# Hyena long convolution on one Trainium2 core: the sums of the filter products moved from GpSimd to VectorE, and the even tiles' products fed from PSUM

## The chip, the cores and the metric

The kernel runs on one core of a Trainium2 chip. The core has a matrix engine (TensorE, PE in the profile; its weight loads are PEld), a vector engine (VectorE, DVE), a scalar engine (ScalarE, ACT), a general engine (GpSimd, POOL) and a queue engine (SyncE, SP) that issues almost all DMA transfers. Each engine works through its own instructions in a fixed order and waits for others on semaphores. The metric is the device time of one execution in microseconds (us).

## The reference, cut to what matters

The program is one encoder block: two token mixers side by side (an S5 state space model and a Hyena operator), merged by gates, then a SwiGLU channel mixer. The change lies in the Hyena operator:

```python
def _fft_conv(z, kf, bias):
    zf = jnp.fft.rfft(zf32, n=2 * seq, axis=1)
    y = jnp.fft.irfft(zf * kf[None], n=2 * seq, axis=1)[:, :seq]
    return (y + zf32 * bias.astype(jnp.float32)).astype(z.dtype)
...
    z = v
    for o in range(HY_ORDER):
        z = gates[o] * _fft_conv(z, kf[:, o], bias[o])
```

The sequence has 1024 positions, there are 512 Hyena channels and two orders, and all is float32. What matters is the product `zf * kf` of a complex spectrum with a complex filter spectrum: for each frequency two real numbers times two real numbers, four products and two sums.

## The kernel before, in words

The Fourier transforms are matrix products on PE. The 512 channels are two halves of 256 columns (`hyena_half`, L505). Each half runs `long_conv` (L480) twice, once per order. A generator per half yields after each step, and `side_by_side` (L535) takes the two in turn, so that one half's waits can be covered by the other. The tile framework then orders the instructions of each engine by priority and by its own timeline of costs (`schedule_with_timeline_sim=True`), so the order on an engine is not the order of the source.

One `long_conv` does this:

* `fold` (L278) adds and subtracts rows of the signal until its even and odd parts can be transformed apart. It uses VectorE, GpSimd (L308, L309, L316, L317, L325, L326) and ScalarE.
* For the four even frequency tiles (7, 6, 4, 5), `spectrum` (L366) makes the tile's real and imaginary part by two to four matmuls into one PSUM tile of [128, 2, 256], named `sp`. There is one such PSUM buffer for each half. ScalarE copies it to the SBUF tile X (L487), and `times_filter` (L460) multiplies it with the filter spectrum `kt`, which SP loads from DRAM (L464, two buffers).
* `times_filter` works on X in SBUF. VectorE makes t2, the two parts crossed times the filter's imaginary part (L466, t in the profile), and X times the filter's real part in place (L473; for tile 7 two halves, L470 and L471). GpSimd then makes the two sums, each [128, 256], into Y (L475 and L476). Y is the input of the inverse transform's matmuls (L413 and L428 through L362), or of `butterfly` (L379) for odd tiles.
* For the odd tiles (0 to 3), `spectrum_odd` (L391) copies one PSUM tile to X (L399) and combines it with a second one out of PSUM on VectorE (L384, L385, L388). `times_filter` then works on X as above, and `butterfly` makes g from two Y tiles.
* `combine_odd` (L440) transforms back and joins the parts, with GpSimd at L454 and L457 and VectorE at L450 and L456.

After each order the result is multiplied with a gate (L517, L529, L530). Over two halves and two orders there are 16 even and 16 odd products, thus 64 sums.

During the Hyena stage the other engines' spare time is filled with two pieces that do not need its result: the gate projections `emit_gates_b` (L1244, PE tile gp) and the S5 branch `emit_branch_a` (L1301, PE tile br, VectorE L1318, weights split by ScalarE L135 and GpSimd L136 into wh and wl). When both halves are done, `emit_merge` (L1329) runs the Hyena branch projection, also named br.

Of the kernel before, what the change touches and what calls it, by code (L numbers as in the profile page):

```python
# [11 lines left out]
ALU = mybir.AluOpType  # L12
# [4 lines left out]
P = 128  # L17
# [336 lines left out]
def transform(E, out, offs, rhs, start, stop, shared=False):  # L354

    n = len(offs)
    if len(rhs[0]) == 2:
        lhs = [(E.dft_hi[:, o:o + P], E.dft_lo[:, o:o + P]) for o in offs]
        mm3(E, out, lhs, rhs, start, stop, shared)
        return  # L360
    for i in range(n):
        E.nc.tensor.matmul(out=out, lhsT=c32(E, offs[i]), rhs=rhs[i][0], start=start and i == 0,  # L362
                           stop=stop and i == n - 1, skip_group_check=shared)


def spectrum(E, sp, ft, parts):  # L366

    out = sp()
    for i in range(2):
        z = parts["even"][i]  # L370
        if ft < 6:
            offs, tiles = [A2_OFF + 256 * kt + P * (ft - 4) for kt in range(2)], range(2)
        else:
            offs, tiles = [M_OFF + P * ((A1, D2), (S4, S2))[i][ft - 6]], [ft - 4]
        transform(E, out[:, i], offs, [tuple(t[:, k] for t in z) for k in tiles], True, True)
    return out


def butterfly(E, out, a, b, special, eng):  # L379

    STT = E.nc.vector.scalar_tensor_tensor
    if special:
        e = col(E.tab, T_E)
        STT(out=out[0], in0=b, scalar=e, in1=a, op0=ALU.mult, op1=ALU.add)  # L384
        STT(out=out[1], in0=a, scalar=e, in1=b, op0=ALU.mult, op1=ALU.subtract)  # L385
    else:
        for o, op in zip(out, (ALU.add, ALU.subtract)):
            eng.tensor_tensor(out=o, in0=a, in1=b, op=op)  # L388


def spectrum_odd(E, sp, k, parts, out):  # L391

    for m in range(2):
        pt = sp()
        for i in range(2):
            transform(E, pt[:, i], [A5_OFF + 512 * m + 256 * n + P * k for n in range(2)],
                      [tuple(t[:, 2 * m + n] for t in parts["odd"][i]) for n in range(2)], True, True)
        if m == 0:
            E.nc.scalar.copy(out[1], pt)  # L399
        else:  # L400
            butterfly(E, out, out[1], pt, k == 0, E.nc.vector)


def combine_even(E, room, inv, product):

    nc = E.nc
    TT = nc.vector.tensor_tensor
    banks = []
    for ft, mats in ((7, (D2T, S2T)), (6, (A1, S4))):
        Y = product(ft)  # L410
        bank = inv("EA")
        for i in range(2):
            transform(E, bank[:, i], [M_OFF + P * mats[i]], [(Y[:, i],)], i == 0, i == 1, True)  # L413
        banks.append(bank)
        yield
    m4 = room("fq", [P, 2, 256], "m4")
    nc.scalar.copy(m4, banks[1])
    m3 = room("t2", [P, 2, 256], "m3", bufs=2)
    nc.scalar.copy(m3, banks[0])
    G = [room("g", [P, 2, 256], "G", bufs=4) for _ in range(2)]  # L420
    nc.gpsimd.tensor_tensor(out=G[0], in0=m3, in1=m4, op=ALU.add)
    TT(out=G[1], in0=m3, in1=m4, op=ALU.subtract)
    EC, ES = inv("EC"), inv("ES")
    for kt in range(2):
        Y = product(4 + kt)
        for bank, i in ((EC, 0), (ES, 1)):
            for t in range(2):
                transform(E, bank[:, t], [A2_OFF + 256 * kt + P * t], [(Y[:, i],)],  # L428
                          kt == 0 and t == 0, kt == 1 and t == 1, True)
        yield  # L430
    ce, so = room("ze", [P, 4, 256], "ce"), room("fw", [P, 4, 256], "so")
    for n in range(2):
        TT(out=ce[:, n], in0=EC[:, n], in1=G[n][:, 0], op=ALU.add)
        TT(out=ce[:, 3 - n], in0=G[n][:, 0], in1=EC[:, n], op=ALU.subtract)
        TT(out=so[:, 2 * n], in0=ES[:, 1 - n], in1=G[n][:, 1], op=ALU.add)
        TT(out=so[:, 3 - 2 * n], in0=ES[:, 1 - n], in1=G[n][:, 1], op=ALU.subtract)
    return ce, so


def combine_odd(E, room, inv, g, ce, so, y):  # L440

    V = E.nc.vector
    for i, z in enumerate((so, ce[:, 3::-1])):
        U, W = inv("U"), inv("W")
        for m, bank in enumerate((U, W)):
            for n in range(2):
                transform(E, bank[:, n], [A5T_OFF + 512 * m + 256 * k + P * n for k in range(2)],
                          [(g[k][m][:, i],) for k in range(2)], n == 0, n == 1, True)
        for out, own, other, t in ((z[:, 0:2], U, W, T_NTAN), (z[:, 3:1:-1], W, U, T_TAN)):
            V.tensor_tensor(out=out, in0=own, in1=out, op=ALU.add)  # L450
            tmp = room("t2", [P, 2, 256], "tw", bufs=2)
            for n in range(2):
                E.nc.scalar.mul(tmp[:, n], other[:, n], col(E.tab, t + n))
            E.nc.gpsimd.tensor_tensor(out=out, in0=out, in1=tmp, op=ALU.add)  # L454
        yield
    V.tensor_tensor(out=y[:, 0:4], in0=ce, in1=so, op=ALU.add)  # L456
    E.nc.gpsimd.tensor_tensor(out=y[:, 7:3:-1], in0=ce, in1=so, op=ALU.subtract)  # L457


def times_filter(E, room, X, o, hf, ft):  # L460

    nc = E.nc
    kt = room("kt", [P, 2, 256], bufs=2)
    nc.sync.dma_start(out=kt, in_=E.kspec[o, hf, ft, :, 0:2])  # L464
    t2 = room("t2", [P, 2, 256], bufs=2)
    nc.vector.tensor_tensor(out=t2, in0=X[:, ::-1], in1=kt[:, 1:2].to_broadcast([P, 2, 256]), op=ALU.mult)  # L466
    if ft == 7:
        k2 = room("k2", [P, 256])
        nc.sync.dma_start(out=k2, in_=E.kspec[o, hf, ft, :, 2])
        nc.vector.tensor_tensor(out=X[:, 0], in0=X[:, 0], in1=kt[:, 0], op=ALU.mult)  # L470
        nc.vector.tensor_tensor(out=X[:, 1], in0=X[:, 1], in1=k2, op=ALU.mult)  # L471
    else:
        nc.vector.tensor_tensor(out=X, in0=X, in1=kt[:, 0:1].to_broadcast([P, 2, 256]), op=ALU.mult)  # L473
    Y = room("Y", [P, 2, 256], bufs=2)
    nc.gpsimd.tensor_tensor(out=Y[:, 0], in0=X[:, 0], in1=t2[:, 0], op=ALU.add)  # L475
    nc.gpsimd.tensor_tensor(out=Y[:, 1], in0=X[:, 1], in1=t2[:, 1], op=ALU.subtract)  # L476
    return Y


def long_conv(E, room, inv, sp, T, o, hf, out):  # L480

    parts = fold(E, room, T, T)
    yield

    def even(ft):
        X = room("t1", [P, 2, 256], "X", bufs=2)
        E.nc.scalar.copy(X, spectrum(E, sp, ft, parts))  # L487
        return times_filter(E, room, X, o, hf, ft)

    ce, so = yield from combine_even(E, room, inv, even)  # L490
    g = []
    for k in range(2):
        X = [room("t1", [P, 2, 256], "X", bufs=2) for _ in range(2)]
        spectrum_odd(E, sp, k, parts, X)
        yield
        Y = [times_filter(E, room, X[n], o, hf, 2 * k + n) for n in range(2)]
        g.append([room("g", [P, 2, 256], bufs=4) for _ in range(2)])
        butterfly(E, g[k], *Y, k == 0, E.nc.vector)
        yield
    y = out()  # L500
    yield from combine_odd(E, room, inv, g, ce, so, y)
    return y
# [1413 lines left out]
```

## Time and profile before

| what | value |
|---|---|
| time, median of 3 runs | 1694.34 us (1690.42 to 1696.2) |
| the profiled execution's own time | 1695.38 us |
| span of its trace, first to last instruction | 1693.6 us |
| PE busy | 1539.2 us (91%) |
| VectorE busy | 1316.4 us (78%) |
| ScalarE busy | 743.4 us (44%) |
| GpSimd busy | 577.6 us (34%) |
| TensorE clock granted, mean | 0.966 |

Times in the trace are counted from the span's start. A busy share over the whole span mixes many stages; the Hyena stage lies from about 660 to 866 us. In a list of groups the numbers after the bar are the total busy time in us, the mean duration of one instruction in ns, and the idle time of the engine just before, with what ended it. An instruction that follows another directly on VectorE starts some 0.08 us before the profile ends the one before it, so the sum of durations is larger than the busy time.

### The profile page before, as it was taken

How to read it: one execution, taken by the hardware profiler on the slowest of the kernel's cores; microseconds unless marked ns; L12 is line 12 of the kernel's file. 1: busy time of each engine (PE TensorE's matmuls, PEld its weight loads, DVE VectorE, ACT ScalarE, POOL GpSimd, SP SyncE). 2: the span in 40 equal slices, each digit the busy share in tenths (PEclk: the TensorE clock that was granted, in tenths of full speed). 3: DMA queues.
4: the chain of work that ended last, by engine and by line, in shares of the span. 5: the costliest groups of instructions: out<-in, count | busy, mean ns of one | idle time of the engine just before them, and what ended most of it. 6: DMA issues, size and time to landing. Idle time of an engine off the chain costs nothing. (4 is left out here: it accounts for less than half of the span.)

```text
span 1693.6 us, 22059 instructions
## 1 busy us (share of the span) xinstructions
PE 1539.2 (91%) x7598; PEld 1272.2 (75%) x7598; DVE 1316.4 (78%) x1967; ACT 743.4 (44%) x1366; POOL 577.6 (34%) x393
## 2 busy tenths in 40 slices
PE   6777889899988898997789998999999999999995
PEld 2666768787777786785578997878888888778884
DVE  6889798889999737898887666866776766578966
ACT  5846456435555464223133465433333333345544
POOL 3355663413334347779631120211111111012232
PEclk9998999999999999999989998999999999999998
DMA  9446653353332276754237732423223332598863
GB/s 327 125 139 190 172 168 103 104 153 99 88 86 63 84 207 248 254 168 138 86 126 258 256 95 63 143 81 106 94 93 105 119 126 87 167 372 311 311 205 113
DMA packets 244871, 263.82 MB, mean 156 GB/s; under 512 B 27672, under 2 KB 168816, under 8 KB 243317
## 3 DMA queue, kind: packets, MB, share of 16 engines
q1 hardware_dynamic: 244278, 259.99, 47.8%
q0 software_dynamic: 480, 2.42, 0.4%
q8 instruction: 60, 0.98, 0.2%
q14 instruction: 53, 0.43, 0.1%
HBM read 195.00 MB, written 67.34 MB: 155 GB/s over the span
## 5 line engine op out<-in xcount | busy, mean ns | idle before, releaser
L136 POOL TENSOR_TENSOR wl<-wf,wh 128x1024 fp32r<-128x1024 f32 (+1 forms) x56 | 129.7, 2317 | 227.8 <-ACT wh L135 167.2
L144 PE MATMUL pj<-hT,wh 128*128 128x512 f32 x480 | 193.5, 403 | 9.0 <-ACT cva L1187 8.3
L146 PE MATMUL pj<-hT,wl 128*128 128x512 f32 x480 | 192.3, 401 | 0.5 <-POOL wl L136 0.5
L146 PE MATMUL gu<-h2T,op 128*128 128x512 f32 x440 | 172.6, 393 | 3.8 <-DVE op L136 3.8
L144 PE MATMUL gu<-h2T,op 128*128 128x512 f32 x440 | 171.3, 393 | 4.5 <-ACT op L135 2.5
L136 POOL TENSOR_TENSOR wl<-wg,wh 128x1024 fp32r<-128x1024 f32 x22 | 55.6, 2533 | 346.9 <-ACT wh L135 346.9
L145 PE MATMUL gu<-h2T,op 128*128 128x512 f32 x440 | 172.7, 392 | 0.0
L135 ACT CAST op<-ws 128x512 fp32r<-128x512 f32 x88 | 54.4, 622 | 182.9 <-PE gu L146 109.0
L145 PE MATMUL dn<-dop 128*128 128x512 f32 x308 | 120.8, 392 | 0.3 <-POOL dop L136 0.3
L146 PE MATMUL dn<-dop 128*128 128x512 f32 x308 | 120.7, 392 | 0.0
L144 PEld LDWEIGHTS pj<-hT,wh 128*128 128x128 f32 x480 | 92.7, 193 | 28.4 <-ACT cva L1187 9.0
L144 PE MATMUL dn<-dop 128*128 128x512 f32 x308 | 111.9, 391 | 2.1 <-ACT dop L135 2.1
L146 PEld LDWEIGHTS pj<-hT,wl 128*128 128x128 f32 x480 | 92.6, 193 | 20.5 <-POOL wl L136 1.4
L145 PE MATMUL pj<-hT,wh 128*128 128x512 f32 x256 | 101.1, 395 | 0.0
L144 PEld LDWEIGHTS gu<-h2T,op 128*128 128x128 f32 x440 | 83.5, 190 | 23.4 <-ACT op L135 3.2
L146 PEld LDWEIGHTS gu<-h2T,op 128*128 128x128 f32 x440 | 83.5, 190 | 22.5 <-DVE op L136 5.0
L145 PEld LDWEIGHTS gu<-h2T,op 128*128 128x128 f32 x440 | 83.6, 190 | 17.1
L145 PE MATMUL pj<-lT,wh 128*128 128x512 f32 x224 | 90.8, 405 | 0.0
L136 POOL TENSOR_TENSOR dop<-bf,dop 128x512 fp32r<-128x512 f32 x17 | 32.0, 1884 | 129.5 <-ACT dop L135 120.9
L1538 DVE TENSOR_TENSOR ws<-wu 128x512 f32<-128x512 f32 x22 | 24.7, 1123 | 66.0 <-DMA wu<-in_ffn_w_gu_dram 66.0
L144 PE MATMUL wop<-woh,mT 128*128 128x256 f32 x256 | 73.0, 285 | 1.6 <-DVE tmp L1413 1.6
L145 PE MATMUL wop<-wol,mT 128*128 128x256 f32 x256 | 72.5, 283 | 0.0
(462 smaller groups left out, 4383.8 us busy)
## 6 DMA issues: line engine op xcount, KB each, us to landing
bf<-in_ffn_w_down_dram SPq DMA_DIRECT2D x105, 256.0 KB
wf<-in_w_in_dram SPq DMA_DIRECT2D x36, 512.0 KB
ada<-in_ada_w_dram SPq DMA_DIRECT2D x48, 256.0 KB
wg<-in_ffn_w_gu_dram SPq DMA_DIRECT2D x22, 512.0 KB
wu<-in_ffn_w_gu_dram SPq DMA_DIRECT2D x22, 512.0 KB
adS<-S SPq DMA_DIRECT2D x44, 256.0 KB
af<-adS SPq DMA_DIRECT2D x44, 256.0 KB
adA<-a SPq DMA_DIRECT2D x33, 256.0 KB
```

The lines of the kernel that those rows point to most:

```text
L135: E.nc.scalar.copy(hi, src)
L136: (lo_eng or E.nc.vector).tensor_tensor(out=lo, in0=src, in1=bc(hi), op=ALU.subtract)
L144: E.nc.tensor.matmul(out=out, lhsT=lh, rhs=rh, start=first, stop=False, skip_group_check=shared)
L145: E.nc.tensor.matmul(out=out, lhsT=lh, rhs=rl, start=False, stop=False, skip_group_check=shared)
L146: E.nc.tensor.matmul(out=out, lhsT=ll, rhs=rh, start=False, stop=last, skip_group_check=shared)
L1538: V.tensor_tensor(out=s1, in0=u1, in1=u2, op=ALU.add)
```

## The change

The function `times_filter` gets one more argument, S, from which the products read; X stays the tile that they are written to. For even tiles S is the PSUM tile of `spectrum`, and ScalarE's copy to X is gone. For odd tiles S is X itself, as before. The two sums into Y are issued on VectorE where they were issued on GpSimd.

```diff
-def times_filter(E, room, X, o, hf, ft):
+def times_filter(E, room, S, X, o, hf, ft):
...
-    nc.vector.tensor_tensor(out=t2, in0=X[:, ::-1], in1=kt[:, 1:2].to_broadcast([P, 2, 256]), op=ALU.mult)
+    nc.vector.tensor_tensor(out=t2, in0=S[:, ::-1], in1=kt[:, 1:2].to_broadcast([P, 2, 256]), op=ALU.mult)
     if ft == 7:
...
-        nc.vector.tensor_tensor(out=X[:, 0], in0=X[:, 0], in1=kt[:, 0], op=ALU.mult)
-        nc.vector.tensor_tensor(out=X[:, 1], in0=X[:, 1], in1=k2, op=ALU.mult)
+        nc.vector.tensor_tensor(out=X[:, 0], in0=S[:, 0], in1=kt[:, 0], op=ALU.mult)
+        nc.vector.tensor_tensor(out=X[:, 1], in0=S[:, 1], in1=k2, op=ALU.mult)
     else:
-        nc.vector.tensor_tensor(out=X, in0=X, in1=kt[:, 0:1].to_broadcast([P, 2, 256]), op=ALU.mult)
+        nc.vector.tensor_tensor(out=X, in0=S, in1=kt[:, 0:1].to_broadcast([P, 2, 256]), op=ALU.mult)
     Y = room("Y", [P, 2, 256], bufs=2)
-    nc.gpsimd.tensor_tensor(out=Y[:, 0], in0=X[:, 0], in1=t2[:, 0], op=ALU.add)
-    nc.gpsimd.tensor_tensor(out=Y[:, 1], in0=X[:, 1], in1=t2[:, 1], op=ALU.subtract)
+    nc.vector.tensor_tensor(out=Y[:, 0], in0=X[:, 0], in1=t2[:, 0], op=ALU.add)
+    nc.vector.tensor_tensor(out=Y[:, 1], in0=X[:, 1], in1=t2[:, 1], op=ALU.subtract)
     return Y
...
         X = room("t1", [P, 2, 256], "X", bufs=2)
-        E.nc.scalar.copy(X, spectrum(E, sp, ft, parts))
-        return times_filter(E, room, X, o, hf, ft)
+        return times_filter(E, room, spectrum(E, sp, ft, parts), X, o, hf, ft)
...
-        Y = [times_filter(E, room, X[n], o, hf, 2 * k + n) for n in range(2)]
+        Y = [times_filter(E, room, X[n], X[n], o, hf, 2 * k + n) for n in range(2)]
```

## Rows read from the trace of the kernel before

**Rows 1.** The chain of waits, 560 to 868 us: start us, us, what.

```profile
863.74 1.97 PE yT L526 x8
```

**Rows 2.** Busy time by stretch: PE, PEld, DVE, ACT, POOL (count), PE clock, DMA share, GB/s.

```profile
660.00:866.00 206.00, 174.80 (x738) 140.92 (x737) 176.11 (x215) 54.63 (x111) 152.38 (x124) 0.95 0.52 170
...
700.00:745.00 45.00, 45.00 (x205) 38.36 (x204) 40.67 (x55) 8.36 (x17) 29.44 (x28) 1.00 0.59 192
...
770.00:800.00 30.00, 22.18 (x84) 16.79 (x83) 27.29 (x25) 9.22 (x18) 27.14 (x20) 0.89 0.45 142
800.00:845.00 45.00, 33.47 (x138) 26.14 (x136) 38.98 (x60) 7.15 (x15) 30.54 (x32) 0.95 0.27 82
...
866.00:905.00 39.00, 39.00 (x174) 31.73 (x173) 29.94 (x41) 13.05 (x21) 7.63 (x6) 0.98 0.60 186
```

**Rows 3.** Who waited for whom on DVE, 660 to 866 us: total us, times, longest.

```profile
DVE g L384 <- POOL Y L476: 5.1, 4, 1.7
DVE t L466 <- ACT X L487: 4.7, 3, 2.0
...
DVE g L388 <- POOL Y L476: 2.0, 2, 1.3
DVE t L466 <- POOL Y L476: 1.9, 2, 1.3
...
DVE X L384 <- POOL Y L476: 1.3, 1, 1.3
```

**Rows 4.** Groups, 660 to 866 us: sums, copy; the last row 770 to 800 us.

```profile
L475 POOL TENSOR_TENSOR Y<-X,t 128x256 f32<-128x256 f32 x32 | 30.1, 940 | 26.4 <-DVE X L473 24.8 <-DVE X L470 1.6
L476 POOL TENSOR_TENSOR Y<-X,t 128x256 f32<-128x256 f32 x32 | 29.2, 911 | 0.0
...
L487 ACT COPY X<-sp 128x512 f32<-128x512 f32 x16 | 9.3, 582 | 23.1 <-PE sp L362 16.5 <-POOL Y L476 6.6
...
L475 POOL TENSOR_TENSOR Y<-X,t 128x256 f32<-128x256 f32 x3 | 3.1, 1040 | 0.4 <-DVE X L470 0.4
```

**Rows 5.** Timeline of DVE and of POOL around 846 us: start us, us, what.

```profile
846.81 3.36 DVE L456 TENSOR_TENSOR yy<-ce,so 128x1024 f32<-128x1024 f32 x1
...
846.41 2.67 POOL L457 TENSOR_TENSOR yy<-ce,so 128x1024 f32<-128x1024 f32 x1
```

**Rows 6.** Groups on DVE, 660 to 866 us: a product that reads PSUM.

```profile
L388 DVE TENSOR_TENSOR X<-X,sp 128x512 f32<-128x512 f32 x8 | 5.5, 683 | 0.8 <-PE sp L362 0.7
```

**Rows 7.** Groups on DVE: 660 to 700, then 770 to 800, then 660 to 866 us.

```profile
L466 DVE TENSOR_TENSOR t<-X,kt 128x512 f32<-128x512 f32 x6 | 10.5, 1757 | 4.1 <-ACT X L487 2.7 <-POOL Y L476 1.3
L473 DVE TENSOR_TENSOR X<-X,kt 128x512 f32<-128x512 f32 x4 | 4.6, 1139 | 0.1
...
L466 DVE TENSOR_TENSOR t<-X,kt 128x512 f32<-128x512 f32 x5 | 9.1, 1818 | 2.6 <-ACT X L487 2.0 <-POOL Y L476 0.6
...
L473 DVE TENSOR_TENSOR X<-X,kt 128x512 f32<-128x512 f32 x2 | 1.8, 919 | 0.0
...
L470 DVE TENSOR_TENSOR X<-X,kt 128x256 f32<-128x256 f32 x4 | 4.0, 999 | 0.2
...
L471 DVE TENSOR_TENSOR X<-X,k 128x256 f32<-128x256 f32 x4 | 2.7, 682 | 0.0
```

**Rows 8.** Groups on DVE, 700 to 745 us.

```profile
L473 DVE TENSOR_TENSOR X<-X,kt 128x512 f32<-128x512 f32 x10 | 8.5, 869 | 0.0
L466 DVE TENSOR_TENSOR t<-X,kt 128x512 f32<-128x512 f32 x10 | 8.2, 826 | 0.0
L388 DVE TENSOR_TENSOR g<-Y 128x512 f32<-128x512 f32 x4 | 5.8, 1495 | 0.7 <-POOL Y L476 0.7
...
L384 DVE SCALAR_TENSOR_TENSOR g<-Y,tab 128x512 f32<-128x512 f32 x2 | 3.6, 1794 | 2.1 <-POOL Y L476 2.1
```

**Rows 9.** Timeline of DVE, two small operations back to back: start us, us, what.

```profile
809.98 0.42 DVE L433 TENSOR_TENSOR ce<-EC,G 128x256 f32<-128x256 f32 x1
810.31 0.41 DVE L434 TENSOR_TENSOR ce<-G,EC 128x256 f32<-128x256 f32 x1
```

## The prediction

> **What bounds the kernel now.** I looked first for where the changed lines run. All 32 products, and with them all 64 sums on GpSimd and the 16 copies on ScalarE, lie in the Hyena stage, so I read that stage alone. The chain of waits enters the Hyena stage only at its end, with the transposes of the last result at 863.7 us [rows 1]; behind it PE is busy for the whole of the next 39 us (the last row of [rows 2]). What ends the Hyena stage earlier should therefore shift all that follows by as much, and the question is only how long the stage from 660 to 866 us becomes.
>
> The busy times by stretch [rows 2] show what limits it. Over the 206 us VectorE is busy for 176.1 us, PE for 174.8, GpSimd for 152.4, ScalarE for 54.6. From 700 to 745 us PE has no gap at all, since the fill work is there. From 770 to 845 us it has gaps of 19.4 us, while VectorE is busy for 66.3 of 75 us. So the stage is held by VectorE and by the short waits between it and GpSimd: VectorE stands idle for 206.0 - 176.1 = 29.9 us in all, of which 5.1 + 2.0 + 1.9 + 1.3 = 10.3 us end with a sum on GpSimd and 4.7 us with ScalarE's copy [rows 3]. I take VectorE's busy time plus its idle time as the length of the stage, and cost each part on that account.
>
> A part of the 176.1 us is no work. The first thing to see is a pair on the timeline [rows 5]: VectorE's L456 starts at 846.81 us while GpSimd's L457 runs from 846.41 to 849.08, and it ends at 850.17, 1.09 us behind GpSimd's end, although it is shown as 3.36 us long. An operation on VectorE with two SBUF inputs stood still while GpSimd worked on SBUF. The second thing is a group that does not do so: L388 with one input in PSUM takes 0.683 us on average over eight instructions [rows 6], in the same stretches in which the filter products out of SBUF, of the same shape, take up to 1.82 us on average [rows 7].
>
> **The change part by part.**
>
> **The copy.** 16 copies of 0.58 us leave ScalarE [rows 4]. ScalarE is busy for a quarter of the stage, so the time itself is worth nothing; what goes is VectorE's wait for it, 4.7 us [rows 3].
>
> **The even products out of PSUM.** From 660 to 700 and from 770 to 800 us all products are even ones: 11 operations t, 6 operations X of full width and 8 halves for tile 7. They cost 10.5 + 4.6 + 9.1 + 1.8 + 4.0 + 2.7 = 32.7 us [rows 7]. With one input in PSUM I price them by the nearest rows: 17 of 0.683 us [rows 6] and 8 of 0.42 us, which is what an operation of 256 columns with a PSUM input takes [rows 9], together 15.0 us. That takes away 17.7 us. The other 5 t and 6 X of even tiles lie where t takes 0.826 and X 0.869 us [rows 8], so 5 x 0.14 + 6 x 0.19 = 1.8 us more. Sum: -19.5 us. Bounds: if reading PSUM does not spare the standstill, 0; nothing better than -19.5, since the price is that of an undisturbed operation. I take the full -19.5, because no instruction of rows 6 shows the standstill.
>
> [...]
>
> **The sums.** GpSimd loses 64 operations, 59.3 us [rows 4], and VectorE gains them. Back to back, operations of 256 columns start 0.33 us apart [rows 9]: 64 x 0.33 = 21.1 us. But X and t2 both lie in SBUF, so the sums can be held by GpSimd's other work. From below this is 0. From above, the nearest row is that of the tile 7 halves, 256 columns with both inputs in SBUF: (4.0 + 2.7) / 8 = 0.84 us, 0.42 us over the undisturbed operation [rows 7, 9]; 64 x 0.42 = 26.9 us. From 660 to 700 us there are 6 products [rows 7], from 700 to 745 us 10 [rows 8], from 770 to 800 us 3 pairs of sums [rows 4], and the other 13 of the 32 behind 800 us. I take 0.42 us for the 18 sums of the first and the third stretch, where GpSimd also has the folds: 7.6 us. For the other 46, t and X from 700 to 745 us show 0.17 us on average with GpSimd busy for 29.4 of 45 us [rows 2, 8]. Some 18.5 us of that are the 20 sums of this stretch themselves (at 0.93 us [rows 4]), so without them GpSimd is busy for a quarter of the time instead of two thirds, and I take 0.17 x 0.25 / 0.65 = 0.065 us: 3.0 us. Sum: +21.1 + 10.6 = +31.7 us.
>
> **What the sums no longer hold up.** The operations on g wait at GpSimd's doings too: 2 x (1.79 - 0.74) + 4 x (1.50 - 0.68) = 5.4 us from 700 to 745 us [rows 6, 8], with an estimate of 0.74 us for L384 undisturbed, a little over the 0.68 of rows 6. The like comes again from 800 to 845 us. Part of this is due to weight splits and L454, which stay on GpSimd. I take -4 us, between 0 and -9.
>
> **The waits of VectorE.** The 10.3 us for a sum and the 4.7 us for the copy go [rows 3]: -15.0 us. Two others may come. The spectrum of the next even tile needs the one PSUM buffer of its half, which the copy freed after 0.58 us and which now stays taken until X is made. The next spectrum is two to four matmuls on PE. What covers it on VectorE is the pair of sums, 0.66 us, and the other half's work. I cost it at 0. Without that cover it would be some 0.6 us for each of the 12 even tiles that follow another of their convolution, 7 us. PE's queue is strictly ordered, so fill matmuls behind a late spectrum would wait too; PE has 31 us of gaps in the stage to take that up [rows 2]. SP's loads of kt wait for the last reader of the old kt, which is X as before, so their order does not change.
>
> **The sum.** VectorE busy: 176.1 - 19.5 + 31.7 - 4.0 = 184.3 us. Idle: 29.9 - 15.0 = 14.9 us. Stage: 199.2 instead of 206.0 us, -6.8 us. The profiled execution took 1695.4 us, 1.0 us over the median of the runs shown, 1694.3. So 1695.4 - 6.8 = 1688.6 us. About 0.3%, or 5 us, is what a measurement of this kernel can tell from no change; the forecast is just beyond it.
>
> **The rivals.**
>
> *The sums are held by GpSimd as much as the products were* (slower). The standstill that the products leave is taken up by the sums, which come right behind them and have two SBUF inputs; GpSimd still has 60 operations and 93 us of work in the stage [rows 2, 4]. If every sum pays 0.42 us, VectorE is busy for 200.6 us and the stage is 215.5 us: 1704.9 us. It decides from about 0.27 us a sum, where the gain is gone. For it: rows 5 and the halves of rows 7. Against it: in the odd part GpSimd has little else left. [...] Chance 0.25.
>
> *The waits only change their name* (no change). VectorE's sums add 31.7 us, the products give back 23.5, and if half of the 15.0 us of idle time returns as waits for a spectrum or for `fold`, the stage is 206.0 + 8.2 - 7.5 = 206.7 us: 1696 us against the profiled execution, 1695 against the median. For it: from 800 to 845 us VectorE has 6.0 us of idle time only, and 26 sums of 0.33 us are 8.6 us. Chance 0.30.
>
> *GpSimd is freed so far that nothing holds the sums* (faster, more). Without the 10.6 us the time is 1678 us. For it: the sums' own share of rows 2. It is counted with the forecast; together 0.45.
>
> **How the numbers follow.** Forecast with its upper variant 0.45, no change 0.30, slower 0.25. The forecast's own range is 1677 to 1689 us, from the sums unheld to where the difference from the median is 0.3%. The range for 8 in 10 has the same lower end and reaches up to 1702 us, which takes in no change and the larger part of the way to the slower rival.
>
> **What the profile of the changed kernel would show.** Right: L466 and L473 fed from sp at 0.68 us with no long ones among them; the sums on VectorE at a mean of at most 0.6 us; the yT transposes of the last result near 857 us; VectorE busy for some 184 us of the stage; no VectorE wait that names L475 or L476. The slower rival: sums with a mean of 0.7 us or more, long ones beside L136, L325, L326, L454. The other: new VectorE waits for PE sp or PE waits for X of an even tile, of 7 us and more. Wrong altogether would be a changed order of instructions, since the framework orders each engine by its own costs: then the fill work or the two halves would stand otherwise against each other than here, and the account by terms would not hold.

## The result and the profile after

The changed kernel takes 1703.35 us (median of 4 runs, 1702.05 to 1704.81) against 1693.68 us before (4 runs, 1690.42 to 1696.2): ratio 1.0057, 95% interval 1.0039 to 1.0075. It is slower by more than the 0.3% that can be told from no change; 1688.6 us was forecast, and the range ended at 1702. The profiled execution took 1702.05 us, with a span of 1700.3 us and a mean granted clock of 0.961 (0.966 before).

First the end of the Hyena stage, in the chain of waits of the changed kernel (start us, us, what). It answers to [rows 1]: 870.44 in place of 863.74.

```profile
870.44 1.64 PE yT L525 x8
```

The last transpose starts at 871.8 us in place of 865.3, and the span ends 6.7 us later: what follows the stage has only moved. The stage has got longer.

The groups on VectorE from 658 to 872 us of the changed kernel answer to [rows 4, 6, 7, 8] (busy us, mean ns, then VectorE's idle time before them).

```profile
L476 DVE TENSOR_TENSOR Y<-X,t 128x256 f32<-128x256 f32 x32 | 20.8, 651 | 0.0
L475 DVE TENSOR_TENSOR Y<-X,t 128x256 f32<-128x256 f32 x32 | 20.3, 634 | 0.2
L466 DVE TENSOR_TENSOR t<-sp,kt 128x512 f32<-128x512 f32 x16 | 10.9, 683 | 3.6 <-PE sp L362 3.6
...
L466 DVE TENSOR_TENSOR t<-X,kt 128x512 f32<-128x512 f32 x16 | 10.6, 681 | 0.0
...
L473 DVE TENSOR_TENSOR X<-sp,kt 128x512 f32<-128x512 f32 x12 | 8.1, 679 | 0.0
```

The even products out of PSUM take 0.68 us each, none of them held, as forecast. The 64 sums show 41.1 us. Each overlaps the next by 0.08 us, so they cost about 41.1 - 64 x 0.08 = 36.0 us, against 31.7 forecast.

VectorE's waits from 658 to 872 us, which answer to [rows 3] (us in total, times, longest us):

```profile
DVE ce L433 <- PE EC L362: 7.3, 3, 2.8
DVE ce L450 <- ACT tw L453: 4.2, 3, 2.0
DVE t L466 <- PE sp L362: 3.6, 3, 2.5
DVE so L450 <- ACT tw L453: 3.2, 2, 2.7
```

No wait for a sum or for the copy is left. But these 18.3 us have come, where the kernel before has 0.7 us of `ce L450 <- ACT tw` and 0.7 us or less of each of the others.

For what follows I cut the stage at four events that each trace shows: the early half's first fold (L299, ze<-T), the late half's fold for order 1 (the last L299), the late half's last g (L388), and the start of the last yT transpose. The early half is half 0, whose order 1 ends first, and the late half is half 1. Busy time by stretch, before (start:end, us, then PE, PEld, DVE, ACT, POOL, PE clock, DMA share, GB/s):

```profile
672.30:779.40 107.10, 96.66 (x419) 78.57 (x418) 94.61 (x106) 27.84 (x58) 83.01 (x66) 0.98 0.63 209
779.40:843.48 64.08, 50.60 (x205) 39.46 (x203) 55.43 (x77) 15.16 (x31) 47.18 (x46) 0.95 0.35 109
843.48:865.30 21.82, 14.54 (x60) 11.97 (x61) 18.43 (x27) 6.63 (x14) 14.44 (x8) 0.74 0.20 72
672.30:865.30 193.00, 161.80 (x682) 130.00 (x681) 168.46 (x208) 49.64 (x103) 144.63 (x118) 0.94 0.49 160
```

The same stretches of the changed kernel:

```profile
670.70:782.36 111.66, 100.83 (x441) 81.84 (x439) 98.02 (x141) 24.41 (x52) 55.01 (x38) 0.99 0.63 208
782.36:851.81 69.45, 51.76 (x200) 40.86 (x200) 64.59 (x113) 12.79 (x27) 20.45 (x15) 0.87 0.28 91
851.81:871.80 19.99, 12.54 (x43) 9.76 (x44) 8.80 (x16) 4.51 (x11) 8.37 (x5) 0.76 0.18 65
670.70:871.80 201.10, 165.13 (x684) 132.46 (x683) 171.41 (x267) 41.71 (x89) 83.83 (x58) 0.92 0.47 153
```

Over the whole, VectorE's busy time rises by 3.0 us only, less than forecast (8.2), but its idle time rises from 24.5 to 29.7 us, where 15.0 us were to go. The first part grows by 4.6 us, and there PE is busy for nine tenths of the time in both kernels; PE's share of that growth is 4.2 us, since 22 more matmuls lie in it. The second part grows by 5.4 us, and there VectorE is at 93%.

The timeline of VectorE in the changed kernel shows what it does there, ahead of the late half's last g (start us, us, what):

```profile
840.93 0.68 DVE L466 TENSOR_TENSOR t<-X,kt 128x512 f32<-128x512 f32 x1
841.53 3.36 DVE L456 TENSOR_TENSOR yy<-ce,so 128x1024 f32<-128x1024 f32 x1
844.81 0.68 DVE L466 TENSOR_TENSOR t<-X,kt 128x512 f32<-128x512 f32 x1
845.41 1.28 DVE L473 TENSOR_TENSOR X<-X,kt 128x512 f32<-128x512 f32 x2
846.62 0.41 DVE L528 TENSOR_TENSOR x<-yT,x 128x256 f32<-128x256 f32 x1
...
849.61 0.41 DVE L476 TENSOR_TENSOR Y<-X,t 128x256 f32<-128x256 f32 x1
849.95 0.68 DVE L136 TENSOR_TENSOR zl<-x,zh 128x512 fp32r<-128x512 f32 x1
850.55 0.41 DVE L528 TENSOR_TENSOR x<-yT,x 128x256 f32<-128x256 f32 x1
...
851.81 1.29 DVE L388 TENSOR_TENSOR g<-Y 128x512 f32<-128x512 f32 x2
```

t, X, Y and g are the late half's; yy, x and zl belong to the early half, which is already at its end. Between t and g stand its L456, eight gate products (L528, L529) and two splits (L136): 3.3 + 8 x 0.33 + 2 x 0.6 = 7.1 us. In the kernel before, g stood ahead of all of these (yy at 846.81 [rows 5]):

```profile
843.48 3.41 DVE L388 TENSOR_TENSOR g<-Y 128x512 f32<-128x512 f32 x2 [1.30 <-POOL Y L476]
```

The framework had ordered VectorE anew. That end of the late half is what the rest of the program waits for.

### The profile page after: what moved, and what is told of

The parts are those of the page before. It is cut to its first block, busy times and chain, and to the rows that moved or that the text cites. A ratio compares the mean times of both kernels' runs of the same rounds, so it can differ in the third digit from the quotient of the medians.

```text
span 1700.3 us, 22016 instructions
## 1 busy us (share of the span) xinstructions
PE 1543.5 (91%) x7598; PEld 1275.0 (75%) x7598; DVE 1321.6 (78%) x2031; ACT 735.3 (43%) x1350; POOL 520.3 (31%) x329
## 5 line engine op out<-in xcount | busy, mean ns | idle before, releaser
L136 POOL TENSOR_TENSOR wl<-wf,wh 128x1024 fp32r<-128x1024 f32 (+1 forms) x56 | 127.2, 2272 | 260.6 <-ACT wh L135 217.9
L136 POOL TENSOR_TENSOR wl<-wg,wh 128x1024 fp32r<-128x1024 f32 x22 | 54.2, 2468 | 348.8 <-ACT wh L135 348.8
L146 PEld LDWEIGHTS pj<-hT,wl 128*128 128x128 f32 x480 | 93.2, 194 | 20.4 <-POOL wl L136 1.2
L136 POOL TENSOR_TENSOR dop<-bf,dop 128x512 fp32r<-128x512 f32 x17 | 41.1, 2424 | 126.2 <-ACT dop L135 115.7
L1537 DVE TENSOR_TENSOR ws<-wu 128x512 f32<-128x512 f32 x22 | 26.1, 1189 | 64.1 <-DMA wu<-in_ffn_w_gu_dram 64.1
L135 ACT CAST wh<-wf 128x1024 fp32r<-128x1024 f32 (+1 forms) x56 | 49.9, 892 | 53.9 <-PE br L145 24.6
```

The source lines that it names most:

```text
L135: E.nc.scalar.copy(hi, src)
L136: (lo_eng or E.nc.vector).tensor_tensor(out=lo, in0=src, in1=bc(hi), op=ALU.subtract)
L146: E.nc.tensor.matmul(out=out, lhsT=ll, rhs=rh, start=False, stop=last, skip_group_check=shared)
L1537: V.tensor_tensor(out=s1, in0=u1, in1=u2, op=ALU.add)
```

## The experiments

Each theory names what would make the loss. **H**: GpSimd holds the sums, so VectorE needs too long for them. **B**: the PSUM buffer is held too long. **O**: VectorE's order puts finished work ahead of the late half's last g. Later **F**: PE's order puts too much fill work into a full part. "Order edge" below means an ordering without a wait, written once:

```diff
-        butterfly(E, g[k], *Y, k == 0, E.nc.vector)
+        E.last_g[hf] = butterfly(E, g[k], *Y, k == 0, E.nc.vector)
...
-    V.tensor_tensor(out=y[:, 0:4], in0=ce, in1=so, op=ALU.add)
+    with E.tc.issue_after(E.last_g[1].ins) if late else nullcontext():
+        V.tensor_tensor(out=y[:, 0:4], in0=ce, in1=so, op=ALU.add)
```

`butterfly` returns its last instruction, and `late` is the early half's order 1. All ratios are to the kernel before.

**1. The sums alone.**

Against the kernel before; ScalarE's copy stays:

```diff
-    nc.gpsimd.tensor_tensor(out=Y[:, 0], in0=X[:, 0], in1=t2[:, 0], op=ALU.add)
-    nc.gpsimd.tensor_tensor(out=Y[:, 1], in0=X[:, 1], in1=t2[:, 1], op=ALU.subtract)
+    nc.vector.tensor_tensor(out=Y[:, 0], in0=X[:, 0], in1=t2[:, 0], op=ALU.add)
+    nc.vector.tensor_tensor(out=Y[:, 1], in0=X[:, 1], in1=t2[:, 1], op=ALU.subtract)
```

> Only the sums move to VectorE; ScalarE still copies the even spectra to SBUF and the products read them there. Theory H (GpSimd holds the sums: 0.64 us each in the changed kernel where 0.41 is undisturbed, 15 us over 64 sums): the products are held as before and the sums on top of it, so 6 to 15 us slower than the kernel before, sums at 0.6 us or more. Theory B (the one PSUM buffer of a half stays taken until the product is made, PE's queue stops behind it): the buffer is freed by the copy again, so within 3 us of the kernel before. Theory O (VectorE's order puts the early half's last steps ahead of the late half's last product): depends on the order that the framework makes; if the early half's L456 again stands ahead of the late half's last g, 5 us or more slower.

Measured: 1703.64 us, ratio 1.0056 (1.0037 to 1.0074). With the sums alone the loss is as large, and since the copy frees the PSUM buffer here, B does not make it. The sums' means are 0.555 and 0.552 us, but now the products behind them are the long ones (t 1.02 us on average).

**2. The even products out of PSUM alone.** Against the changed kernel:

```diff
-    nc.vector.tensor_tensor(out=Y[:, 0], in0=X[:, 0], in1=t2[:, 0], op=ALU.add)
+    nc.gpsimd.tensor_tensor(out=Y[:, 0], in0=X[:, 0], in1=t2[:, 0], op=ALU.add)
```

and the same for the second sum.

> Only the even products read PSUM; the sums stay on GpSimd. H: the products lose their 19.5 us of standing still and no sums come to VectorE, so 5 to 12 us faster than the kernel before. B: PE stops behind the taken buffer for 5 to 8 us as in the changed kernel, so no faster than the kernel before, up to 6 us slower. O: as the order comes out; if the late half's last g stands ahead of the early half's L456, no slower than the kernel before.

Measured: 1691.87 us, ratio 0.999 (0.9974 to 1.0005). H expected 5 to 12 us of gain, and it did not come. Here too yy (833.33 us), six gate products and two splits stand ahead of the late half's last g (842.13 us), yet nothing is lost against the kernel before. So this order need not cost anything by itself: with the sums on GpSimd, VectorE would have had to wait for them there (5 shows that wait).

**3. The changed kernel with the order edge.**

> The changed kernel with one edge of order added on VectorE: the early half's last L456 is queued behind the late half's last g. O: the late half's last g comes some 7 us earlier (845 instead of 852 us) and the kernel is 5 to 7 us faster than the changed one, 1696 to 1698 us. H and B: the time goes elsewhere, within 2 us of the changed kernel, 1701 to 1705 us.

Measured: 1693.41 us, ratio 0.9997 (0.9983 to 1.0011). The whole loss is gone. The timeline of VectorE in this kernel, the same place:

```profile
842.84 3.43 DVE L468 TENSOR_TENSOR t<-X,kt 128x512 f32<-128x512 f32 x2
846.19 1.28 DVE L475 TENSOR_TENSOR X<-X,kt 128x512 f32<-128x512 f32 x2
...
848.85 1.29 DVE L388 TENSOR_TENSOR g<-Y 128x512 f32<-128x512 f32 x2
850.06 1.22 DVE L458 TENSOR_TENSOR yy<-ce,so 128x1024 f32<-128x1024 f32 x1
```

The fold-to-g stretch is 62.0 us (786.81 to 848.85) in place of 69.45, shorter than the 64.1 us of the kernel before. The two t, together 3.43 us, have taken over the standstill that yy had: GpSimd's half of yy runs beside them (842.90 to 845.72 us). The sums are held nearly as in the changed kernel (0.634 and 0.620 us against 0.634 and 0.651), and the time is back all the same, so the held sums are not what the whole change loses by:

```profile
L477 DVE TENSOR_TENSOR Y<-X,t 128x256 f32<-128x256 f32 x32 | 20.3, 634 | 0.2
L478 DVE TENSOR_TENSOR Y<-X,t 128x256 f32<-128x256 f32 x32 | 19.8, 620 | 0.0
```

**4. Even sums with one input in PSUM.**

```diff
-        X = room("t1", [P, 2, 256], "X", bufs=2)
-        return times_filter(E, room, spectrum(E, sp, ft, parts), X, o, hf, ft)
+        S = spectrum(E, sp, ft, parts)
+        return times_filter(E, room, S, S, o, hf, ft)
```

> The changed kernel, but the even tiles' product with the filter's real part is written back into its PSUM tile, so that the even tiles' sums have one input in PSUM and one in SBUF. The buffer is then taken until the sums are made. H: the 32 even sums fall to 0.42 us (from 41.1 us in all for the 64 to 29 or less), VectorE gains 12 us in the two stretches of the even tiles and the kernel is 5 to 10 us faster than the changed one. B: the buffer is freed 0.7 us later for each even tile, PE's stops grow, the kernel is 2 to 8 us slower than the changed one. O: within 2 us of the changed one unless the order changes.

Measured: 1718.07 us, ratio 1.0148 (1.0127 to 1.0169). Groups on VectorE, 670 to 886 us:

```profile
L475 DVE TENSOR_TENSOR Y<-sp,t 128x256 f32<-128x256 f32 x15 | 6.3, 420 | 0.3
L476 DVE TENSOR_TENSOR Y<-sp,t 128x256 f32<-128x256 f32 x15 | 6.2, 413 | 0.0
```

And PE's waits from 670.55 to 885.80 us in the same kernel:

```profile
PE EA L362 <- DVE Y L475: 10.1, 4, 6.3
PE U L362 <- DVE g L388: 9.4, 2, 7.4
```

The even sums are as free as can be, and the kernel is the slowest of all, where H expected it to be faster. But the buffer is held longer here, in step with B, and the late half's g (865.93 us) stands 15 us behind the early half's yy (850.81 us), so this run prices neither H nor B by itself.

**5 and 6. The order edge on each half of the change.** The edits of 2 and of 1, each with the edge.

> The kernel before with the even tiles' products out of PSUM (sums stay on GpSimd) and with the order edge: the early half's last y L456 of order 1 is queued on VectorE behind the late half's last g. Without the edge the same edit took 1691.9 us and had the early half's last steps ahead of the late half's last product. Theory O (that order is what costs): the time falls by 4 to 7 us against it, to 1685-1688, late half's last g ahead of the early half's y, end of the yT transposes some 5 us sooner against the fold at the stage's head. Theory B (the PSUM buffer held until X is made, PE's queue stopped behind it): within 2 us of 1692, with PE's waits for X as long as in the kernel without the edge. Theory H (GpSimd holds VectorE's sums) has no sums on VectorE here, so it gives less than before by the products' gain alone and nothing for the edge.

> The kernel before with the 64 sums on VectorE (ScalarE's copy stays) and with the order edge. Without the edge this edit alone took 1703.6 us, ratio 1.0056, and had the early half's y L456 ahead of the late half's last g too. Theory O: the ratio falls to 0.998-1.002 (1691-1697 us), since the order is all that it loses. Theory H: the sums' 35 us on VectorE (64 x 0.55) are what costs; the edge gives back 2 us or less and the time stays at 1701 or more. In between (1697-1700): both have a part.

Measured: 1690.91 us, 0.9982 (0.9972 to 0.9992), and 1700.93 us, 1.0039 (1.0026 to 1.0051). The edge gives 1.0 and 2.7 us here, with intervals that overlap: less than O expected. In 5 the place of yy and the gate products is taken by a wait of 2.65 us for GpSimd's sums. With the sums on VectorE alone the loss mostly stays, near what H expected (1701 us or more): the order does not explain it there. The whole stage in busy times, first of 5, then of 6:

```profile
674.74:867.10 192.36, 161.47 (x685) 130.82 (x685) 146.56 (x208) 41.89 (x89) 133.90 (x118) 0.93 0.48 160
```

```profile
671.95:873.00 201.05, 164.32 (x681) 132.15 (x680) 180.10 (x270) 50.07 (x103) 94.95 (x58) 0.91 0.47 152
```

The first is the row to remember. In 5, VectorE works 21.9 us less than before (146.56 against 168.46), and the stage is 0.6 us shorter (192.36 against 193.00). Traces are single executions, so 0.6 us is no measure by itself, but the two other traces with the products alone agree: 193.4 us in 2 and 193.5 us in 12 (with holds on the fill, below).

**7. The bad order alone.** Only the late half's last step is issued later and queued behind the early half's yy.

```diff
-    V.tensor_tensor(out=y[:, 0:4], in0=ce, in1=so, op=ALU.add)
+    E.early = V.tensor_tensor(out=y[:, 0:4], in0=ce, in1=so, op=ALU.add)
...
-        butterfly(E, g[k], *Y, k == 0, E.nc.vector)
+        if o == 1 and hf == 1 and k == 1:
+            yield
+            yield
+            yield
+            with E.tc.issue_after(E.early.ins):
+                butterfly(E, g[k], *Y, k == 0, E.nc.vector)
+        else:
+            butterfly(E, g[k], *Y, k == 0, E.nc.vector)
```

> The kernel before, products and sums and copy where they were, with only the order turned over: the late half's last g of order 1 is issued three steps later and queued on VectorE behind the early half's last y L456. Nothing else is computed elsewhere. Theory O: this alone costs about what the edge gave back to the changed kernel, +5 to +9 us, 1699-1703 us, late half's last g behind 847 us on the profile's scale and the yT transposes that much later. Theories H and B: sums and PSUM buffers are as before, so the time is within 3 us of before (1691-1697 us).

Measured: 1696.75 us, ratio 1.0015 (1.0004 to 1.0026): a loss, but 2.4 us of the 5 to 9 expected. VectorE's timeline shows a milder order than the changed kernel's: only yy got ahead of g, and none of the gate products.

```profile
844.87 1.23 DVE L456 TENSOR_TENSOR yy<-ce,so 128x1024 f32<-128x1024 f32 x1 [3.73 <-POOL ce L454]
846.01 3.44 DVE L388 TENSOR_TENSOR g<-Y 128x512 f32<-128x512 f32 x2
849.37 0.41 DVE L536 TENSOR_TENSOR x<-yT,x 128x256 f32<-128x256 f32 x1
```

**8. Even sums back on GpSimd, with the edge.**

```diff
+    add = E.nc.gpsimd if ft >= 4 else E.nc.vector
-    nc.vector.tensor_tensor(out=Y[:, 0], in0=X[:, 0], in1=t2[:, 0], op=ALU.add)
+    add.tensor_tensor(out=Y[:, 0], in0=X[:, 0], in1=t2[:, 0], op=ALU.add)
```

and the same for the second sum.

> The changed kernel with the order edge, and with the sums of the even tiles 4 to 7 given back to GpSimd, whose folds run in the same stretch; the odd tiles' sums stay on VectorE. Theory H: the even tiles' sums are those that GpSimd's folds hold up (some 10 us of VectorE time over their undisturbed 0.41 us), so this beats the changed kernel with the edge (1693.4) by 4 to 8 us: 1685-1689. Theory O alone: the order was all, the time stays within 2 us of 1693. Theory B: even products still hold their PSUM buffer, PE's waits for X stay, time within 3 us of 1693.

Measured: 1698.98 us, ratio 1.0028 (1.0013 to 1.0042). By the medians it is slower than 3, where all sums are on VectorE, though H expected 4 to 8 us less. VectorE's busy time fell from 170.5 to 161.1 us between the first fold and the last transpose without a gain: the stage is as long in both traces (194.7 and 194.8 us). Where the 5.6 us between the medians lie, these two traces do not show.

**9 to 12. The fill on PE.** Counted in PE's instruction stream, 288 fill matmuls (gp and br) are mixed into the stage. The kernel before has 125 of them ahead of the first U and 264 ahead of the early half's second even spectrum (tile 6) of order 1. The changed kernel, and 3, have 137 and 288; 5 has 133 and 276. The expectations below name the late half's first spectrum for the second count, and that is a misreading: by the traces all 288 stand ahead of that one in the kernel before too. The first hold therefore puts the last 24 later than the kernel before has them, and no run restores its exact order. So F: the sums' new costs made the framework pull fill forward, into the part where PE is full. The holds are edges too:

```diff
+    HOLD = (14, (1, 1, 7)), (12, (1, 0, 7)), (6, (0, 1, 1)), (3, (0, 0, 1))
...
+            behind = next((m for first, m in HOLD if 2 * c + th >= first), None)
+            with E.tc.issue_after(E.mark[behind].ins) if behind else nullcontext():
+                branch(E, pt, w, z, th)
-            branch(E, pt, w, z, th)
```

`E.mark` keeps the last matmul of a spectrum by order, half and tile (or k). Number 9 has the first hold only.

> The changed kernel with the order edge, and the last 24 of the 288 fill matmuls (gp and br) of the Hyena stage held on PE behind the late half's first spectrum of order 1, where the kernel before has them (264 ahead of that spectrum; the changed kernel, with the edge or without, has all 288 ahead). Theory F: part of the loss of the sums on VectorE is that the framework puts more fill ahead of the late half on a full PE; held back it lies in PE's gaps of the last stretch. Then the time from the early half's first fold to the late half's fold of order 1 falls from 112.7 us by 3 to 6 us, the last stretch grows by less, and the kernel takes 1687-1691 against 1693.4 with the edge alone. Rival S: the fill's place does not matter, PE's work is the same and comes back in the last stretch; 1692-1696.

> As the kernel before it, but with four holds: fill from the 133rd on behind the early half's second odd spectrum of order 0, from the 169th on behind the late half's, from the 241st on behind the early half's first spectrum of order 1, the last 24 behind the late half's. The early half's first inverse transform of the odd part then stands behind 132 fill matmuls, not 137 (kernel before 125). Theory F: 1686-1691, at or below the kernel with one hold. Rival S: 1692-1696.

> The kernel before with the 64 sums on VectorE, ScalarE's copy kept, the order edge, and the same four holds of the fill. Without the holds it took 1700.9 us and had all 288 ahead of the late half's first spectrum of order 1. Theory F: 1694-1698. Rival S, with theory H (what is left is VectorE's time for the sums): 1699 or more.

> The kernel before with the even products out of PSUM, sums on GpSimd, the order edge, and the same four holds. Without the holds it took 1690.9 us with 276 fill matmuls ahead of the late half's first spectrum of order 1, 24 of them now go behind. Theory F: 1686-1690. Rival S: 1690-1693.

Measured: 9: 1694.67 us, 0.9998 (0.9982 to 1.0014). 10: 1692.59 us, 0.9993 (0.9978 to 1.0008). 11: 1696.29 us, 1.0013 (0.9999 to 1.0026). 12: 1691.55 us, 0.9987 (0.9973 to 1.0). On the changed kernel (9, 10) and on the products alone (12) the holds give nothing; most of what leaves the first part comes back in the second, as rival S (the fill's place does not matter) said; in 9 the first part fell by 1.5 us only (112.7 to 111.2). Stretches of 10:

```profile
671.20:778.75 107.55, 98.97 (x425) 81.68 (x423) 97.68 (x141) 24.02 (x51) 55.08 (x37) 0.97 0.64 212
778.75:844.09 65.34, 47.40 (x198) 37.50 (x198) 60.09 (x102) 11.25 (x24) 20.96 (x16) 0.95 0.31 96
```

Against 3, the first part is 5.2 us shorter (107.55 for 112.71), the second 3.3 us longer (65.34 for 62.04). On the sums alone (11 against 6) the holds gave 4.6 us, with intervals that just touch; as they changed other orders along, I leave open why there.

**13 to 15. Half of the edge, and both ends again on one chip.** In 13 yy stays ahead of the late half's g, and only the early half's gate products go behind it:

```diff
+            with E.tc.issue_after(E.last_g[1].ins) if hf == 0 else nullcontext():
+                nc.vector.tensor_tensor(out=x2[:, :, 0], in0=yv[:, :, 0], in1=x2[:, :, 0], op=ALU.mult)
-            nc.vector.tensor_tensor(out=x2[:, :, 0], in0=yv[:, :, 0], in1=x2[:, :, 0], op=ALU.mult)
```

and likewise the second product; 14 is the changed kernel itself, 15 is 3 again.

> The changed kernel with half of the order edge: the early half's gate products on yT and what follows them are queued on VectorE behind the late half's last g, but its last y L456 still stands ahead of it. In the changed kernel 7.2 us of the early half's work stand between the late half's last t and its last g (y 3.3, eight gate products 2.7, two splits 1.2); here 3.3 us. Theory O: the loss goes with that work, so about half of the edge's gain: ratio to before 1.002-1.004 (1697-1701 us). Rival: the gain of the edge came from where y stands alone (nothing here, 1.0057), or from the gate products alone (all of it, 1.000).

> The changed kernel itself, beside its two variants on one chip: ratio to before 1.004-1.007.

> The changed kernel with the whole order edge, beside the changed kernel on one chip. Theory O: ratio to before 0.998-1.001 again. If the edge's gain was the chip's or the runs' scatter: 1.004 or more.

Measured: 13: 1694.56 us, 1.0003 (0.9992 to 1.0014). 14: 1701.41 us, 1.0045 (1.0032 to 1.0059). 15: 1692.98 us, 0.9991 (0.9982 to 1.0001). The edge's gain is no scatter, and nearly all of it, 6.9 of 8.4 us, comes with the gate products and the splits behind them alone: the rival in the expectation, not the even split that I expected. VectorE's timeline of 13:

```profile
841.16 3.36 DVE L457 TENSOR_TENSOR yy<-ce,so 128x1024 f32<-128x1024 f32 x1
844.44 0.68 DVE L467 TENSOR_TENSOR t<-X,kt 128x512 f32<-128x512 f32 x1
...
847.25 0.41 DVE L477 TENSOR_TENSOR Y<-X,t 128x256 f32<-128x256 f32 x1
847.70 1.29 DVE L388 TENSOR_TENSOR g<-Y 128x512 f32<-128x512 f32 x2
848.91 0.42 DVE L530 TENSOR_TENSOR x<-yT,x 128x256 f32<-128x256 f32 x1
```

yy is long here, 3.36 us against 1.22 in 3, beside GpSimd's half of it (840.62 to 843.43 us). Moved away, as in 3, it leaves the standstill to the two t (3.43 us in place of 2 x 0.6), so its place costs only about 1 us. From the first of these two t to g it is 7.1 us here, 6.0 us in 3 and 10.9 us in the changed kernel.

The stretches side by side (us, from the events above; cut in each kernel's own trace):

| kernel | fold to fold | fold to last g | g to last yT | sum | ratio |
|---|---|---|---|---|---|
| before | 107.1 | 64.1 | 21.8 | 193.0 | 1 |
| changed | 111.7 | 69.4 | 20.0 | 201.1 | 1.0057 |
| 14, changed again | 112.3 | 67.0 | 19.0 | 198.3 | 1.0045 |
| 3, changed with edge | 112.7 | 62.0 | 20.0 | 194.8 | 0.9997 |
| 15, 3 again | 111.8 | 61.8 | 19.8 | 193.4 | 0.9991 |
| 13, half of the edge | 112.3 | 63.3 | 19.1 | 194.7 | 1.0003 |
| 2, products | 106.2 | 66.9 | 20.3 | 193.4 | 0.999 |
| 5, products, edge | 105.8 | 66.1 | 20.4 | 192.4 | 0.9982 |
| 6, sums, edge | 114.4 | 65.9 | 20.7 | 201.0 | 1.0039 |
| 10, changed, edge, holds | 107.6 | 65.3 | 19.5 | 192.4 | 0.9993 |

The traces are single executions, and those of one kernel differ by 2.8 us (changed, 14) and 1.4 us (3, 15) in the sum. The profiled executions of 14 and 15 are 6.6 us apart (1700.25 and 1693.64), and 4.9 us of that lie in the stage. The rest lies outside it, where the traces scatter by some microseconds (from the start of the last transpose to the end of the span it was 824.1 to 829.6 us in the traces of 2, 3 and 5 to 12), and it is attributed to nothing.

The lowest ratio is that of 5, the products out of PSUM with the sums on GpSimd and the edge. At 0.9982 its interval excludes 1, but 0.2% is less than the 0.3% that can be told from no change, and the intervals of 2, 3, 10, 12 and 15 overlap it.

## Why the prediction was wrong

**Right: the even products.** -19.5 us rested on 0.683 and 0.42 us per operation; measured 0.683 (t), 0.679 (X) and 0.412 (the halves). In 5, which has only this and the edge, VectorE's busy time in the stage falls by 21.9 us.

**Right in kind, 4.3 us too small: the sums.** +31.7 us was forecast and 36.0 measured, as 0.64 us on average shown. That is above the 0.6 that I gave as right and below the 0.7 of the slower rival.

**Right in kind, too small: what the sums no longer hold up.** -4 us was taken; the operations on g fell from 21.0 to 12.5 us, by 8.5. The odd products are hardly held any more either, so that all products together fell from 67.8 to 43.5 us, by 24.3. With the +36.0 us of the sums this makes +3.2 us, where VectorE's busy time rose by 3.0: that side of the account closes.

**Right: the old waits go.** None of [rows 3] that names a sum or the copy is left.

**Wrong, and the step that failed: "Idle: 29.9 - 15.0 = 14.9 us".** I took VectorE's busy and idle time as the length of the stage and let 15.0 us of idle time vanish. It rose by 5.2 us. Two things stand behind it.

The first carries the loss of the whole change: the order. I kept each engine's order and named a new one only as what would make the account "wrong altogether", without a chance or a price. It came. On VectorE 3.8 us of gate products and splits and 3.3 us of yy of the early half got ahead of the late half's last g, the one instruction of the two halves that the end waits for. Queued behind it, they give back 8.4 to 9.9 us by the medians (14 against 15, changed against 3), the gate products and splits alone 6.9. Inside the stage the traces show 4.9 to 6.3 us of that, and 3.6 us for the gate products and splits (14 against 13). The order costs that much in the whole change alone: the edge gives 2.7 us with only the sums moved (6 against 1) and 1.0 us with only the products (5 against 2), both with overlapping intervals.

The second ate the forecast gain: even in a good order the changed kernel is no faster than before (0.9997, 0.9991, 0.9993 in 3, 15, 10). VectorE is not what the whole stage waits for. Up to the late half's fold PE is busy for 90% of the time, and time taken from VectorE there buys next to nothing: in 5 VectorE works 12.7 us less in that part (81.9 against 94.6), and the part is 1.3 us shorter. Over the stage, 21.9 us less gave 0.6 us, and 0.18% of the time. The row for 700 to 745 us in [rows 2] had PE without a gap, and I read it, but then priced the sums and products of that stretch like those behind 800 us. Behind the fold VectorE is at 86% before and at 94% in 3. It has 3.0 us more work there, but its idle time falls from 8.7 to 3.6 us, as the prediction wanted, and the part gets shorter (64.1 to 62.0 us); that is less than the first part loses (107.1 to 112.7).

Open stays the loss of the sums alone. In 6, with the edge, it is still 0.39%, and 7.3 of its 8.1 us of stage lie ahead of the late half's fold (114.4 against 107.1 us). There VectorE has 7.8 us more work, and PE has 18 more matmuls, 4.9 us more; holding the fill back (11) brought the ratio to 1.0013. Which of the two makes that loss, no run separates.

**Costed at 0, and not what decided: the PSUM buffer.** PE waits 7.2 us for X of L473 and 1.1 us for L471 in the changed kernel, above the bound of 7 us. But the first figure is still 6.2 us in 3, where the loss is gone. That a longer hold is dear is in step with 4, which doesn't isolate it; 1, where the copy frees the buffer, loses as much as the whole change.

**The rivals.** "Slower" gave 1704.9 us, close to the result, by a mechanism that did not carry it: the sums paid (36.0 - 21.1) / 64 = 0.23 us each over the undisturbed price, below the 0.27 from which this rival was to decide, and in 3 they pay nearly the same (40.1 against 41.1 us shown) while the loss is gone. "Waits only change their name" is the nearest in kind: after the order is mended it is what is left. VectorE's idle time in the stage is 24.3 us in 3 and 22.6 us in 15, against 24.5 before, though the waits of [rows 3] for a sum or the copy are gone. The bound of 1702 us was 1.35 us too low, since no case priced a changed order.

## What to carry to other kernels

Where a framework orders the queues by its own costs, moving an operation to another engine can reorder what stands around it: compare the order of the instructions before pricing, and look at what now stands ahead of the last instruction of the path that ends the stage. Price an edit in each stretch by the engine that is full there; here 12.7 us of work taken from VectorE were worth 1.3 us in a part where PE was busy for 90% of the time. If a change that should help is slower, queue single instructions behind the critical one before undoing the change.

## What the runs showed of the hardware

In these runs the operations on VectorE that read one input from PSUM took no longer beside GpSimd, and some with both inputs in SBUF did. In the changed kernel 18 of the 36 even products, out of PSUM, ran beside an instruction of GpSimd for more than 0.1 us, and none of the 36 took more than 0.69 us. Of the 64 sums, out of SBUF, 16 took more than 0.5 us, up to 2.56 us, and each of these ran beside one; their means were 0.63 and 0.65 us. In 4 the even sums, with one input in PSUM, took 0.42 and 0.41 us on average, and none of them more than 0.43, while the odd sums of the same kernel, out of X in SBUF, took 0.45 and 0.69 and up to 1.52. What was new to me is that such a standstill was passed on: in the changed kernel yy took 3.36 us beside GpSimd's half of it (840.99 to 843.81 us), and in 3, where the late half's two t stood in its place, they took 3.43 us beside that half and yy 1.22 us. Moving the one that showed it saved about 1 us there (7.1 us from the first t to g in 13, 6.0 in 3).

Reading PSUM cost nothing at 512 elements: 0.683 us against 0.681 for the same product out of SBUF, both in the changed kernel.
